# The gated MLP's up projection by seven half-size products instead of eight, its down projection as a phase of its own

## The chip, the cores and the metric

The kernel runs on one core of a Trainium2 chip. The time is device microseconds (us) of one execution of the whole program. The engines of a core are TensorE (PE: matrix products; its weight loads are counted apart as PEld), VectorE (DVE), ScalarE (ACT), GpSimd (POOL) and SyncE (SP), which mostly issues DMAs. Each engine works through its own queue in order.

## The reference, cut to what matters

One decoder block on 512 tokens of 2048 channels: a modulated norm, an input projection, a state-space group and an attention group, an output projection, and then the MLP that the change is about, with a final norm:

```python
def conv_ffn(h, w_up, conv_w, conv_b, w_down):
    up = h @ w_up                                  # (512, 2048) @ (2048, 11264)
    up = causal_depthwise_conv_width_3(up, conv_w) + conv_b
    val, gate = jnp.split(up, 2, axis=-1)          # 5632 channels each
    return (jax.nn.silu(gate) * val) @ w_down      # (512, 5632) @ (5632, 2048)
```

Its result is scaled by a modulation vector (section 5 of the modulation `silu(c) @ w_ada`), added to the residual, and normed.

## The kernel before

All activations lie transposed: channels on 128 partitions, 512 tokens along the row. Every f32 product is made of three matmuls of parts: a number is split into hi (`split`, L59: a cast on ACT) and lo (the difference, on DVE), and `mm3` (L85) adds hi·hi, hi·lo and lo·hi in PSUM (its three lines are L87 to L89). Weights come from memory in pieces of 128 x 2048 (1 MB) by `weights` (L67): one DMA on SP into `wr` (two buffers), then two splits of 128x1024 into `wh` and `wl` (two buffers each). Instructions stand in the order of a scheduler with priorities; the weights' loads and splits are put at high priority, and so ahead. What waits for what follows from buffers: a new tile of a name waits until the last reader of the buffer is done.

Phase C (`phase_c`, L1011) is the second half of the output projection. It adds 16 tiles into the residual `x2` (L1025), sums squares for the norm (`add_square`, L944), and beside it makes section 4 of the modulation: a 1 MB load `adw` (on POOL's queue) and a multiply with sum on DVE (L113) for each of 16 tiles. `norm2` (L1007) makes the norm's factors for each half of the tokens, with a power on POOL (L135).

Phase D (`phase_d`, L1074) is the MLP. `up` makes one of 88 tiles of 128 channels: 16 k-tiles of the contraction, three matmuls each of 512 tokens, so 48 matmuls, then `conv` (L1065: one ACT and two DVE instructions from PSUM). A value tile and its gate tile are a pair; Silu on ACT (L1176) and a product on DVE (L1177) join them, and `split` makes `ah` and `al`, which stay in SBUF. The first pair (`up_first`) runs in halves of 256 tokens while `modulate` (L305: two DVE and one ACT instruction) makes its inputs `h2h` and `h2l`. After every four pairs and one more, `down` adds these four k-tiles into all 16 output tiles: 12 matmuls and one DVE add (L1124) each. So up and down alternate eleven times. Section 5 of the modulation is made beside the early pairs. The last eight output tiles (`last`) run in halves of 256 tokens, so that the norm and the output of one lie beside the products of the other.

## Time and profile before

| | |
|---|---|
| three runs | 2459.17, 2460.2 (median), 2462.0 us |
| the profiled execution: span from first to last instruction | 2464.1 us |
| PE busy | 2336.9 us, 95% of the span |
| DVE, ACT, POOL busy | 61%, 37%, 10% |
| mean granted TensorE clock | 0.967 of full speed |
| DMA | 365 MB, 148 GB/s |

The page gives no other time for the profiled execution than its span, which is 3.9 us above the median of the runs. Phase D takes the time from about 971 us to the end. A matmul's record begins when it starts and ends when its modelled pipeline ends, so neighbours overlap: the pitch from start to start is what a matmul costs, not its record's length.

### The profile page before, as it was taken

What the parts mean: (1) busy time and instruction counts of PE and PEld (TensorE: products, weight loads), DVE (VectorE), ACT (ScalarE), POOL (GpSimd) and SP (SyncE); (2) the same over time, 40 slices, a digit from 0 to 9 for tenths busy, and PEclk for the clock granted to TensorE, in tenths of its full rate; (3) what the DMA queues carried; (4) which work ended last, traced back from release to release, by engine and by line L of the source; (5) the groups of instructions that cost most, each with busy time, mean ns of one, the idle gap of its engine ahead of it and who ended that gap; (6) DMA issues with size and microseconds to landing.
All of it is one profiled execution on the core that took longest, in us unless ns stands there. A gap on an engine that the chain in (4) does not pass through costs nothing.

```text
span 2464.1 us, 27445 instructions
## 1 busy us (share of the span) xinstructions
PE 2336.9 (95%) x10574; PEld 1893.2 (77%) x10574; DVE 1496.3 (61%) x2381; ACT 916.2 (37%) x1602; POOL 251.3 (10%) x313
## 2 busy tenths in 40 slices
PE   7689999989899889999999999999999999999997
PEld 5567778866677668888888888888888888888887
DVE  7688877669988887864443444353434444444437
ACT  3223444458768724322322232222222222222225
POOL 7995111100000010000000000000000000000000
PEclk9899999979899999999999999999999999999999
DMA  8675645576566584642222222222222222222222
GB/s 336 241 242 209 220 144 164 172 221 210 167 228 199 181 307 185 228 182 96 92 100 88 102 86 103 86 103 86 103 86 103 86 103 88 101 88 100 91 98 103
DMA packets 85202, 365.20 MB, mean 148 GB/s; under 512 B 18528, under 2 KB 27104, under 8 KB 51152
## 3 DMA queue, kind: packets, MB, share of 16 engines
q1 hardware_dynamic: 75552, 327.82, 38.1%
q0 software_dynamic: 9520, 35.63, 4.3%
q8 instruction: 83, 1.36, 0.2%
q14 instruction: 47, 0.39, 0.0%
HBM read 341.42 MB, written 21.96 MB: 147 GB/s over the span
## 4 chain that ended last, share of the span: by engine, by line
PE 76%; DVE 8%; POOL 5%; issue 5%; ACT 3%; DMA 2%; SPq 0%; POOLq 0%; DVEq 0%; ACTq 0%
PE up L87 13%; PE up L88 13%; PE up L89 13%; PE dn L87 7%; PE dn L89 7%; PE dn L88 7%; PE mm L87 2%; PE mm L89 2%; PE mm L88 2%; POOL stt L337 2%; DVE adw L113 1%; DVE wl L62 1%; PE s L870 1%; PE acc L629 1%; ACT Pt L882 1%
## 5 line engine op out<-in xcount | busy, mean ns | idle before, releaser
L62 DVE TENSOR_TENSOR wl<-wr,wh 128x1024 fp32r<-128x1024 f32 (+1 forms) x360 | 436.6, 1216 | 552.7 <-ACT wh L62 530.9
L62 ACT CAST wh<-wr 128x1024 fp32r<-128x1024 f32 (+1 forms) x362 | 372.1, 1031 | 1037.1 <-PE up L88 588.3
L88 PE MATMUL up<-h2l,wh 128*128 128x512 f32 x1376 | 543.0, 395 | 0.0
L87 PE MATMUL up<-h2h,wh 128*128 128x512 f32 x1376 | 543.0, 395 | 0.0
L89 PE MATMUL up<-h2h,wl 128*128 128x512 f32 x1376 | 543.0, 395 | 0.0
L88 PEld LDWEIGHTS up<-h2l,wh 128*128 128x128 f32 x1376 | 259.3, 188 | 60.5
L89 PEld LDWEIGHTS up<-h2h,wl 128*128 128x128 f32 x1376 | 259.3, 188 | 60.5
L87 PEld LDWEIGHTS up<-h2h,wh 128*128 128x128 f32 x1376 | 259.3, 188 | 60.3
L89 PE MATMUL dn<-ah,wl 128*128 128x512 f32 (+1 forms) x704 | 274.3, 390 | 0.0
L88 PE MATMUL dn<-al,wh 128*128 128x512 f32 (+1 forms) x704 | 274.2, 389 | 0.0
L87 PE MATMUL dn<-ah,wh 128*128 128x512 f32 (+1 forms) x704 | 274.1, 390 | 0.0
L1124 DVE SCALAR_TENSOR_TENSOR x<-dn,mod,x 128x512 f32<-128x512 f32 (+1 forms) x184 | 133.5, 727 | 188.8 <-PE dn L89 186.7
L135 POOL TENSOR_TENSOR rms_r<-rms_v,mhalf 128x2 f32<-128x2 f32 (+1 forms) x8 | 8.9, 1108 | 1658.7 <-DVE rms_v L133 1658.6
L87 PEld LDWEIGHTS dn<-ah,wh 128*128 128x128 f32 x704 | 132.6, 188 | 29.8 <-ACT ah L62 0.3
L88 PEld LDWEIGHTS dn<-al,wh 128*128 128x128 f32 x704 | 132.6, 188 | 29.6
L89 PEld LDWEIGHTS dn<-ah,wl 128*128 128x128 f32 x704 | 132.6, 188 | 29.6
L113 DVE SCALAR_TENSOR_TENSOR adw<-adw,silc 128x2048 f32<-128x2048 f32 x63 | 149.8, 2377 | 5.7 <-DMA adw<-in_wada_dram 5.7
L87 PE MATMUL mm<-yh,wh 128*128 128x512 f32 (+1 forms) x320 | 129.3, 408 | 17.6 <-ACT yh L62 6.2
L88 PE MATMUL mm<-yl,wh 128*128 128x512 f32 (+1 forms) x320 | 128.1, 401 | 3.9 <-DVE yl L62 3.9
L89 PE MATMUL mm<-yh,wl 128*128 128x512 f32 (+1 forms) x320 | 127.4, 400 | 0.3 <-DVE wl L62 0.3
L87 PE MATMUL b<-hh,wh 128*128 128x512 f32 x192 | 67.7, 409 | 24.2 <-ACT hh L238 14.7
L87 PEld LDWEIGHTS mm<-yh,wh 128*128 128x128 f32 x320 | 62.2, 196 | 32.5 <-ACT yh L62 7.5
(400 smaller groups left out, 3450.9 us busy)
## 6 DMA issues: line engine op xcount, KB each, us to landing
wr<-in_wup_dram SPq DMA_DIRECT2D x88, 1024.0 KB, 4.8
adw<-in_wada_dram SPq DMA_DIRECT2D x49, 1024.0 KB, 6.5
wr<-in_wdn_dram SPq DMA_DIRECT2D x44, 1024.0 KB, 4.8
wr<-in_wada_dram SPq DMA_DIRECT2D x32, 1024.0 KB, 5.0
wr<-in_wout_dram SPq DMA_DIRECT2D x16, 1024.0 KB, 6.0
adw<-in_wada_dram POOLq DMA_DIRECT2D x14, 1024.0 KB, 5.7
wr<-in_wp_dram SPq DMA_DIRECT2D x12, 1024.0 KB, 5.6
s5wt<-in_wuT_dram SPq DMA_DIRECT2D x16, 512.0 KB, 4.2
```

The costliest lines, as they stand in the source:

```text
L62: return self.A.copy(hi, src), self.V.tensor_sub(lo, src, hi.bitcast(F32))
L87: self.T.matmul(ps, wh, xh, start=start, stop=False)
L88: self.T.matmul(ps, wh, xl, start=False, stop=False)
L89: self.T.matmul(ps, wl, xh, start=False, stop=stop)
L113: self.V.scalar_tensor_tensor(t, t, 1.0, self.silc, op0=ALU.mult, op1=ALU.mult, accum_out=out)
L135: self.rms_pow = self.nc.gpsimd.tensor_tensor(r[:, 0:n], v[:, 0:n], self.mhalf.to_broadcast([P, n]), op=ALU.pow)
L337: V.tensor_scalar(w, x, c, None, op0=op0)
L629: T.matmul(Y[:, 64 * g:64 * g + 64], w3[:, :, g], U[:, g], start=True, stop=False)
L870: T.matmul(s[:, :c + n], q[hd], K[b][:, i, k0:k0 + c + n], start=i == 0, stop=i == 1)
L882: A.mul(x, x, rs[:, 3 * hd + 1 + b:3 * hd + 2 + b])
L1124: V.scalar_tensor_tensor(x2[:, m, sl], p[:, sl], self.mod[:, 5, m:m + 1], x2[:, m, sl], op0=ALU.mult, op1=ALU.add)
```

## The change

The up projection of a pair is taken as one matrix product of 2 x 2 blocks: the weights of the value tile and the gate tile (rows), each cut into two halves of the contraction (A11, A12 for the value, A21, A22 for the gate), times the input, cut into halves of the contraction and of the tokens. Pairs 2 to 43 of 0 to 43 make its four result blocks by seven products of 8 k-tiles and 256 tokens (Strassen in Winograd's form), so 7 x 8 x 3 = 168 matmuls of 256 tokens. Four sums of input blocks (`t1` to `t4`) are made once, after pair 0. Four sums of weights are made for each pair on DVE (L1193, in place, 128x1024), each of the seven operands is split, and four DVE instructions put the results together (L1216 to L1219) ahead of the convolution. The gate comes out with its sign turned, which a second set of taps (`tapn`) takes back. Pairs 0 and 1 are made by all eight products, in halves of the tokens.

The gated tile goes to memory (`a_d`) by a DMA on POOL's queue. The residual goes there too in phase C (`x2_d`, sixteen tiles on POOL's queue), since its place is needed. The down projection then follows all of up: five rounds of eight k-tiles and a last one of four, the inputs read back and split again. Section 5 of the modulation is made in its first round. `cv` has three buffers instead of five.

```diff
@@ phase_c
         def add(mt, p, sl):
-            V.scalar_tensor_tensor(x2[:, mt, sl], p, self.mod[:, 2, mt:mt + 1], x2[:, mt, sl],
-                                   op0=ALU.mult, op1=ALU.add)
-            self.add_square(self.acc2[:, sl], x2[:, mt, sl], mt == 0, W)
+            x = x2[mt // 4][:, mt % 4, sl]
+            V.scalar_tensor_tensor(x, p, self.mod[:, 2, mt:mt + 1], x, op0=ALU.mult, op1=ALU.add)
+            self.add_square(self.acc2[:, sl], x, mt == 0, W)
+            nc.gpsimd.dma_start(self.x2_d[:, mt, sl], x)
...
+    def gated(self, m, val, gate, neg, W):
+        val, gate = self.conv(val, m, W), self.conv(gate, NFF + m, W, neg)
+        self.A.activation(gate, gate, AF.Silu)
+        self.V.tensor_mul(val, val, gate)
+        self.nc.gpsimd.dma_start(self.a_d[:, m], val)
...
+    def up_first(self, x2, W, R, ps):
...
+                    if c == 0:
+                        x = x2[k // 4][:, k % 4, sl]
+                        gain, shift = self.mod[:, 4, k:k + 1], self.mod[:, 3, k:k + 1]
+                        self.modulated = self.modulate(x, gain, shift, self.rb2[:, sl], hi, lo, None, x)
+                        A.activation(x, x, AF.Identity, bias=shift)
+                    for e in range(2):
+                        wh, wl = w[k // 8][e]
+                        self.mm3(p[:, 2 * e + f], (wh[:, k % 8], wl[:, k % 8]), (hi, lo), k == 0, k == KT - 1)
...
+    def up_rest(self, ps):
...
+            for c in range(2, NFF):
+                with tc.high_priority():
+                    ra = self.wp.tile([P, 2048], F32, name="wr", bufs=2)
+                    nc.sync.dma_start(ra, a["wup"][c])
+                    rb = W.tile([P, 2048], F32, name="wq", bufs=2)
+                    nc.sync.dma_start(rb, a["wup"][NFF + c])
+                a11, a12, a21, a22 = (r[:, 1024 * i:1024 * i + 1024] for r in (ra, rb) for i in range(2))
...
+                def product(out, src, x, add=None):
+                    with tc.high_priority():
+                        if add is not None:
+                            V.tensor_add(src, src, add)
+                        wh, wl = pair(src)
+                    xh, xl = op[x]
+                    for k in range(8):
+                        self.mm3(out, (wh[:, k], wl[:, k]), (xh[:, k], xl[:, k]), k == 0, k == 7)
+
+                product(sb[:, 2], a11, "b11")
+                p1 = W.tile([P, 256], F32, name="p1", bufs=2)
+                A.copy(p1, sb[:, 2])
+                product(sb[:, 0], a12, "b21")
+                product(sa[:, 0], a22, "t4")
+                product(sa[:, 2], a22, "t1", a21)
+                product(sb[:, 1], a22, "t2", a11)
+                product(sa[:, 3], a12, "b22", a22)
+                product(sa[:, 1], a21, "t3", a11)
...
+                V.tensor_add(e[:, 0::2], sb[:, 0:2], two(p1))
+                V.tensor_add(u, sa[:, 1:3], two(e[:, 2]))
+                V.tensor_add(g, sa[:, 0::2], two(u[:, 0]))
+                V.tensor_add(e[:, 1], sa[:, 3], u[:, 1])
+                self.gated(c, e[:, 0:2].rearrange("p a s -> p (a s)"), g.rearrange("p a s -> p (a s)"), True, W)
+
+    def down(self):
...
+            for q in range(4):
+                nc.sync.dma_start(x2[:, 4 * q:4 * q + 4], self.x2_d[:, 4 * q:4 * q + 4])
...
+            def inputs(k0):
+                r = R.tile([P, 4, S], F32, name="ar", bufs=2)
+                nc.sync.dma_start(r, self.a_d[:, k0:k0 + 4])
...
+                    self.split(r[:, i], ah, al)
...
+            for c in range(5):
+                acts = inputs(8 * c) + inputs(8 * c + 4)
...
+                    for q in range(8):
+                        w = self.weights(a["wdn"][c, q])
                         for e in range(2):
+                            if c == 0:
+                                self.ada_rest(5, 2 * q + e, L, 2)
+                            wh, wl = w[e]
+                            add(2 * q + e, lambda k: (wh[:, k], wl[:, k]), acts, whole)
```

Three places show how the instructions move. First DVE in the middle of the up projection. Before, two tiles of a pair stood there like this (`up` is the tile's bank, `wr` the raw weights):

```order
L62 TENSOR_TENSOR wl<-wr,wh 128x1024 x2
L1070 SCALAR_TENSOR_TENSOR cv<-up,taps,cv 128x511
L1071 SCALAR_TENSOR_TENSOR cv<-up,taps,cv 128x510
L62 TENSOR_TENSOR wl<-wr,wh 128x1024 x2
L1070 SCALAR_TENSOR_TENSOR cv<-up,taps,cv 128x511
L1071 SCALAR_TENSOR_TENSOR cv<-up,taps,cv 128x510
L1177 TENSOR_TENSOR cv<-cv 128x512
L62 TENSOR_TENSOR al<-cv,ah 128x512
```

Now a part of one pair's row on DVE (`xh`, `xl` and `wq` are further buffers of weights; `sa` and `sb` hold the seven results; numbers tell buffers apart):

```order
L1216 TENSOR_TENSOR e_9329<-sb_9126,p1_9155 128x2x256
L62 TENSOR_TENSOR wl_9384<-wr_9347,wh_9383 128x1024
L62 TENSOR_TENSOR xl_9412<-wq_9349,xh_9411 128x1024
L1193 TENSOR_TENSOR wq_9349<-wq_9349 128x1024
L1217 TENSOR_TENSOR u_9330<-sa_9125,e_9329 128x512
L1193 TENSOR_TENSOR wq_9349<-wq_9349,wr_9347 128x1024
L62 TENSOR_TENSOR wl_9441<-wq_9349,wh_9440 128x1024
L1218 TENSOR_TENSOR n_9331<-sa_9125,u_9330 128x512
L1193 TENSOR_TENSOR wq_9349<-wq_9349,wr_9347 128x1024
L1219 TENSOR_TENSOR e_9329<-sa_9125,u_9330 128x256
L1193 TENSOR_TENSOR wr_9347<-wr_9347,wq_9349 128x1024
L62 TENSOR_TENSOR xl_9470<-wq_9349,xh_9469 128x1024
```

The sums and splits of the next pair's weights (9347, 9349) stand between the instructions that put this pair's results together.

Second, SP where up ends and down begins, which is new (`ar` is the gated input, `x2` the residual, both from memory):

```order
L1235 DMA ar_18649<-a_d_77 128x2048
L1230 DMA x2_18625<-x2_d_76 128x2048 x4
L1261 DMA silc_18670<-in_cB_dram 128x2048
L72 DMA wr_18889<-in_wdn_dram 128x2048
L106 DMA adw_18684<-in_wada_dram 128x2048
```

Ahead of this row stand three loads of down weights and the first `ar`. Before, SP's queue held only loads of weights there:

```order
L72 DMA wr_9572<-in_wdn_dram 128x2048
L72 DMA wr_9638<-in_wdn_dram 128x2048
L72 DMA wr_9704<-in_wup_dram 128x2048
L72 DMA wr_9767<-in_wup_dram 128x2048
L72 DMA wr_9836<-in_wup_dram 128x2048
```

Thus the inputs of down have come into SP's queue behind the third load of its weights.

## Rows read from the trace of the kernel before

**Rows 1.** The page's head, its part 1 (busy us, share of the span, instructions of each engine) and the first line of its part 4 (the chain of work that ended last, by engine).

```profile
span 2464.1 us, 27445 instructions
PE 2336.9 (95%) x10574; PEld 1893.2 (77%) x10574; DVE 1496.3 (61%) x2381; ACT 916.2 (37%) x1602; POOL 251.3 (10%) x313
PE 76%; DVE 8%; POOL 5%; issue 5%; ACT 3%; DMA 2%; SPq 0%; POOLq 0%; DVEq 0%; ACTq 0%
```

**Rows 2.** Busy time by stretch: bounds and length in us; busy us (instructions) of PE, PEld, DVE, ACT, POOL; granted clock; DMA share; GB/s. The first stretch is of 512-token matmuls, the others of 256-token ones (the last tiles of down, the last two tiles of the output projection).

```profile
1200.00:1500.00 300.00, 300.00 (x1293) 243.28 (x1292) 132.00 (x148) 79.95 (x93) 0.00 (x0) 1.00 0.27 95
2425.70:2435.70 10.00, 10.00 (x85) 10.00 (x84) 8.18 (x17) 6.83 (x15) 0.00 (x0) 1.00 0.00 0
952.10:960.60 8.50, 8.50 (x72) 8.50 (x71) 4.58 (x8) 3.06 (x5) 0.00 (x0) 1.00 0.67 247
```

**Rows 3.** DVE in order of time amid the up projection: start, length in us, line, operation; in brackets the idle time before and what ended it.

```profile
1199.54 1.22 DVE L62 TENSOR_TENSOR wl<-wr,wh 128x1024 fp32r<-128x1024 f32 x1 [4.34 <-ACT wh L62]
1200.68 0.74 DVE L1070 SCALAR_TENSOR_TENSOR cv<-up,taps,cv 128x511 f32<-128x511 f32 x1
1201.46 0.75 DVE L1071 SCALAR_TENSOR_TENSOR cv<-up,taps,cv 128x510 f32<-128x510 f32 x1
...
1211.84 0.75 DVE L1070 SCALAR_TENSOR_TENSOR cv<-up,taps,cv 128x511 f32<-128x511 f32 x1
...
1223.00 0.74 DVE L1070 SCALAR_TENSOR_TENSOR cv<-up,taps,cv 128x511 f32<-128x511 f32 x1
```

**Rows 4.** Groups of instructions of DVE and ACT from 1100 to 2400 us, shapes apart: count, then busy us, mean ns of one, idle us before and what ended it.

```profile
L62 DVE TENSOR_TENSOR wl<-wr,wh 128x1024 fp32r<-128x1024 f32 x234 | 286.7, 1225 | 502.0 <-ACT wh L62 494.2
L1124 DVE SCALAR_TENSOR_TENSOR x<-dn,mod,x 128x512 f32<-128x512 f32 x156 | 117.1, 751 | 185.0 <-PE dn L89 183.5
L1071 DVE SCALAR_TENSOR_TENSOR cv<-up,taps,cv 128x510 f32<-128x510 f32 x77 | 57.6, 748 | 2.4
L62 DVE TENSOR_TENSOR al<-cv,ah 128x512 fp32r<-128x512 f32 x38 | 26.2, 690 | 19.9 <-ACT ah L62 19.9
L62 ACT CAST wh<-wr 128x1024 fp32r<-128x1024 f32 x233 | 244.3, 1049 | 850.4 <-PE up L88 538.9 <-PE dn L88 311.5
L1069 ACT ACTIVATE cv<-up,taps 128x512 f32<-128x512 f32 x77 | 59.6, 774 | 0.0
L1176 ACT ACTIVATE cv<-cv 128x512 f32<-128x512 f32 x38 | 24.0, 632 | 86.5 <-DVE cv L1071 86.5
L62 ACT CAST ah<-cv 128x512 fp32r<-128x512 f32 x38 | 23.5, 619 | 22.0 <-DVE cv L1177 22.0
```

**Rows 5.** PE in order of time: the first and the last of 120 matmuls of 256 tokens in a row, and two that follow on an interruption.

```profile
2425.70 0.28 PE L87 MATMUL dn<-ah,wh 128*128 128x256 f32 x1
...
2439.87 0.28 PE L89 MATMUL dn<-ah,wl 128*128 128x256 f32 x1
...
2440.36 0.37 PE L87 MATMUL dn<-ah,wh 128*128 128x256 f32 x1
2440.56 0.28 PE L88 MATMUL dn<-al,wh 128*128 128x256 f32 x1
```

**Rows 6.** DVE in order of time while the first pair's inputs are modulated, the first of its two instructions for each of three tiles by row.

```profile
984.23 1.26 DVE L308 SCALAR_TENSOR_TENSOR cv<-x,mod,rb 128x256 f32<-128x256 f32 x3
...
986.60 1.27 DVE L308 SCALAR_TENSOR_TENSOR cv<-x,mod,rb 128x256 f32<-128x256 f32 x3
```

**Rows 7.** ACT in order of time in the same place, three tiles by row.

```profile
984.73 1.31 ACT L309 ACTIVATE h2h<-cv,mod 128x256 fp32r<-128x256 f32 x3 [1.06 <-DVE cv L308]
```

**Rows 8.** Phase C: busy time in one stretch, columns as in rows 2.

```profile
880.00:940.00 60.00, 57.75 (x239) 46.18 (x240) 53.85 (x68) 15.49 (x19) 5.92 (x11) 0.96 0.81 300
```

**Rows 9.** POOL in order of time: the issue of one DMA in phase C.

```profile
870.91 0.59 POOL L106 DMA_DIRECT2D adw<-in_wada_dram  x1 [7.82 <-DVE mod L317]
```

**Rows 10.** Busy time in the stretches around a stall of PE, columns as in rows 2.

```profile
875.00:880.00 5.00, 1.83 (x10) 1.53 (x8) 4.04 (x5) 1.99 (x2) 0.54 (x1) 0.51 0.67 247
880.00:885.00 5.00, 3.51 (x8) 2.81 (x9) 5.00 (x9) 1.26 (x2) 0.36 (x1) 0.50 0.93 324
885.00:890.00 5.00, 5.00 (x22) 4.03 (x21) 3.26 (x5) 1.06 (x2) 0.71 (x2) 0.96 0.98 375
```

**Rows 11.** PE in order of time behind that stall, 512-token matmuls.

```profile
881.49 0.76 PE L87 MATMUL mm<-yh,wh 128*128 128x512 f32 x1 [4.66 <-DVE x L1025]
882.05 0.63 PE L88 MATMUL mm<-yl,wh 128*128 128x512 f32 x1
882.48 0.63 PE L89 MATMUL mm<-yh,wl 128*128 128x512 f32 x1
```

**Rows 12.** The page's DMA issues: count, KB each, median us from issue to landing.

```profile
adw<-in_wada_dram SPq DMA_DIRECT2D x49, 1024.0 KB, 6.5
wr<-in_wdn_dram SPq DMA_DIRECT2D x44, 1024.0 KB, 4.8
```

**Rows 13.** The page's group of the modulation's products on DVE, columns as in rows 4.

```profile
L113 DVE SCALAR_TENSOR_TENSOR adw<-adw,silc 128x2048 f32<-128x2048 f32 x63 | 149.8, 2377 | 5.7 <-DMA adw<-in_wada_dram 5.7
```

More of the change, by code (lines that the diff above doesn't have):

```diff
@@ L46 @@
 ADA = [2, 2, 2, 2, 2, 2, 2, 2, 2, 2, 2, 2, 2, 2, 2, 2]
-CVB = 5
+CVB = 3
 M_K, M_C = 0, 512
@@ L109, in ada @@
             self.after([load], self.heads)
-        if sec == 5:
-            self.after([load], self.modulated)
         with self.tc.high_priority(-120 if late else 0):
@@ L1189, in phase_d @@
-            down(*pend)
+            x2 = H.tile([P, KT, S], F32, name="x2")
+            for q in range(4):
+                nc.sync.dma_start(x2[:, 4 * q:4 * q + 4], self.x2_d[:, 4 * q:4 * q + 4])
+            acc = H.tile([P, S], F32, name="acc2")
+            def inputs(k0):
+                r = R.tile([P, 4, S], F32, name="ar", bufs=2)
+                nc.sync.dma_start(r, self.a_d[:, k0:k0 + 4])
+                out = []
+                for i in range(4):
+                    ah, al = (R.tile([P, S], F32R, name=n, bufs=12) for n in ("ah", "al"))
+                    self.split(r[:, i], ah, al)
+                    out.append((ah, al))
+                return out
@@ new lines, in add @@
+            def add(m, w, acts, sl, end=False):
+                p = ps.tile([P, 4, P], F32, name="dn", bufs=6).rearrange("p a b -> p (a b)")[:, sl]
+                n = len(acts)
+                for k in range(n):
+                    self.mm3(p, w(k), [x[:, sl] for x in acts[k]], k == 0, k == n - 1)
+                x = x2[:, m, sl]
+                V.scalar_tensor_tensor(x, p, self.mod[:, 5, m:m + 1], x, op0=ALU.mult, op1=ALU.add)
+                if end:
+                    self.add_square(acc[:, sl], x, m == 0, H)
+                    A.mul(x, x, self.vec(V_GFIN + m))
@@ new lines, in down, with quad @@
+            acts = inputs(40)
+            E = st.enter_context(tc.tile_pool(name="po", bufs=1, reuse_waits="tile"))
+            def quad(w, e):
+                wh, wl = w[e // 2]
+                return lambda k: (wh[:, 4 * (e % 2) + k], wl[:, 4 * (e % 2) + k])
+            for q in range(2):
+                w = self.weights(a["wdl"][q])
+                for e in range(4):
+                    add(4 * q + e, quad(w, e), acts, whole, True)
+            w = [self.weights(a["wdl"][2])]
+            w.append(self.weights(a["wdl"][3], E.tile([P, 4, 8, P], F32R, name="wz")))
@@ new lines, in down, with norm, final @@
+            out = E.tile([P, KT, S], F32, name="out")
+            rb = [None, None]
+            def norm(f):
+                so = slice(256 * f, 256 * f + 256)
+                rb[f] = H.tile([P, S], F32, name="cv", bufs=CVB)[:, 0:256]
+                A.copy(rb[f], self.rms(acc[:, so], C_INVD, ps, "up", 2, 2))
+            def final(f):
+                so = slice(256 * f, 256 * f + 256)
+                k0 = 0
+                for n in ((2,) * 8 if not f else (2, 2, 4, 4, 2, 2)):
+                    k = slice(k0, k0 + n)
+                    V.tensor_mul(out[:, k, so], x2[:, k, so], rb[f].unsqueeze(1).to_broadcast([P, n, 256]))
+                    nc.sync.dma_start(a["out"][:, k, so], out[:, k, so])
+                    k0 += n
@@ L1191, in run @@
+            for f in range(2):
+                for e in range(8):
+                    if f and e == 2:
+                        norm(0)
+                    add(8 + e, quad(w[e // 4], e % 4), acts, slice(256 * f, 256 * f + 256), True)
+            norm(1)
+            final(0)
+            final(1)
     def run(self):
```

241 lines of the change are left out of this document (121 added, 120 removed).

## The prediction

> **What bounds the kernel now.** I read the page's head and chain first: PE holds 76% of the chain that ended last, and is busy 95% of a span of 2464.1 us [rows 1]. Then the busy time by stretch: from 1200 to 1500 us PE is busy 300.00 of 300.00 us at clock 1.00, DVE 132.00, ACT 79.95, DMA share 0.27 [rows 2]. So in the MLP nothing waits ahead of PE, and what counts is the pitch of its matmuls. The convolution's instruction L1070 comes once for each tile of 48 matmuls, at 1200.68, 1211.84 and 1223.00 us [rows 3]: 11.16 us for 48, a pitch of 0.2325 us at 512 tokens. For 256 tokens I take a run of 120 matmuls: the first starts at 2425.70, the last at 2439.87 [rows 5], so 14.17 / 119 = 0.1191 us. In the other such stretch 72 starts fill 8.5 us plus the part of one that hangs over [rows 2], about 0.120. I use 0.1195, with 0.119 and 0.120 as bounds.
>
> **Pairs 2 to 43, the gain.** A pair costs PE 2 x 11.16 = 22.32 us now. Seven products of 8 x 3 matmuls of 256 tokens cost 168 x 0.1195 = 20.08 us (19.99 to 20.16). The gain is 2.24 us a pair, 42 x 2.24 = **94 us** (91 to 98). Seven eighths of the columns would be 19.53; the rest is the dearer half-length matmul.
>
> This holds if DVE keeps up, since its cover shrinks most. By pair it does 7 differences and 4 sums of 128x1024 at 1.225 us = 13.5; four results, three of 512 and one of 256 elements, about 3 x 0.75 + 0.42 = 2.7; four convolution steps at 0.748 = 3.0; one product 0.69 [rows 4]. That is 19.9 us by full durations, against 20.08 of PE. But back to back they overlap: L62 starts at 1199.54 and the next instruction at 1200.68 [rows 3], 1.14 instead of 1.22, which makes 11 x 1.14 = 12.5 and 18.8 in all, 94%. ACT does 7 casts at 1.049, two convolution starts at 0.774, Silu 0.632 and a copy of about 0.4, 9.9 us [rows 4].
>
> DVE works in order, so I follow its row from the moment 0 at which a pair's seventh product ends, with 24 x 0.1195 = 2.87 us a product. The first result that waits for that product (u) stands behind the next pair's third split and first sum. The weights' buffers hold four products, so the third split's cast waits for the sixth product of the pair before, which ends at -2.87: cast to -1.8, split to -0.6, sum to +0.6. So u comes 0.6 us late; nothing on PE waits for it. From there 18.8 - 2.3 = 16.5 us of work are left, to 17.1; the next such cast is there at 20.08 - 1.8 = 18.3. DVE therefore waits about a microsecond in each pair and doesn't fall behind. The fourth product's weights are split at about 3.2 us and wanted at 3 x 2.87 = 8.6: five microseconds of slack, which every later one keeps too. I forecast PE as the bound, DVE with almost no room.
>
> [...]
>
> **Pairs 0 and 1, phase C.** Pair 1 now takes 192 matmuls at 0.1195 = 22.9 instead of 22.3: **+0.6**. Pair 0 is paced by its inputs. DVE takes 2.37 us for three tiles [rows 6]; ACT took 1.31 for three [rows 7] and now does a second instruction on each, 2.6 for three. Over 32 tiles that is up to 32 x 0.08 = 2.6 us; the last ones can come late, and the splits of pair 1's weights now stand behind two new DVE instructions of 1.14 us. I take **+2** (0 to 5). In phase C 4 MB of residual more go to memory. The stretch 880 to 940 moved 300 GB/s at a share of 0.81 [rows 8], so full use would be about 370 GB/s and 4 MB take 11 us, as much as the idle 0.19 x 60 = 11. POOL spends 0.59 us on an issue [rows 9], and one such issue stands ahead of the first half's power for the norm. DVE, at 53.85 of 60, waits for the `adw` loads that share the DMAs. I take **+2** (0 to 8).
>
> **Pair 1 to pair 2.** Here buffers couple the engines. Pair 2's first split needs the buffer that pair 1 reads to its end (0 here). Cast 1.05, split 1.23: the first matmul with the lo weights can start at 2.4, and product 1 ends at 5.2. The second cast stands on ACT behind Silu of pair 1, which waits for four convolution steps on DVE, which stand behind that first split: 2.4 + 4 x 0.77 = 5.5, Silu to 6.2, cast to 7.2, split to 8.4. So PE waits 2.4 and then 3.2; from there PE's 2.87 a product stays behind what is ready. With the clock (below) **+6.5** (3 to 12).
>
> **Up to down.** T is the end of the last up product. SP's queue now has, in this order, the third load of down weights, then the two loads of inputs (`ar`), then the residual. The third load needs the first one's buffer; the second half of that is split into a buffer that product 6 holds to T - 2.87. Cast and split end at about T - 0.5, so `ar` is issued at about T. Where loads queue up a landing takes 6.5 us, alone 4.8 [rows 12]. DVE has its last convolution in front of it until about T + 7.5 anyway. Cast 0.62 and difference 0.69 [rows 4] give a first complete k-tile at about T + 8; then DVE's 0.69 a tile keeps PE's 3 x 0.2325 = 0.70. Bounds: 4.8 + 0.6 = 5, and two loads in a row, 9.6 + 1.3 = 11.
>
> [...] Some 3.5 us at half speed lose 1.75: I take 2 here (0 to 6), so **+10** for this boundary (5 to 17).
>
> **The down phase.** It has the same number of matmuls, and fewer DVE adds (6 instead of 11 a tile), which were covered. Its first round is 384 x 0.2325 = 89 us. Section 5 of the modulation now falls in it: 16 x 2.38 = 38.1 on DVE [rows 13], with 16 splits at 1.23 = 19.7, 16 adds at 0.75 = 12, 8 input differences at 0.69 = 5.5 [rows 4], in all 75: covered, if the loads come. About 10 MB stand ahead of the first modulation load, some 30 us at the rate above, while six banks hold results for 6 x 5.58 = 33 us, from T + 8 to T + 41. I take **+1** (0 to 8). The end of the kernel is as before.
>
> **Sum.** -94 + 0.6 + 2 + 2 + 6.5 + 10 + 1 = -72 us. Against the profiled execution: 2464 - 72 = 2392. The median of the runs is 3.9 lower: **2388 us**. By the favourable ends -98 + 0.6 + 0 + 0 + 3 + 5 + 0 = -89, 2371; by the others -91 + 0.6 + 5 + 8 + 12 + 17 + 8 = -40, 2420.
>
> **Rivals.**
> - *DVE sets the pace without being slower than before.* At full durations 19.9 plus the wait of a microsecond or more for the third cast: 21.2 a pair. For it: 94% leave nothing for a longer instruction. Against: the overlap in rows 3, and the slack of five microseconds. Time: 42 x 1.1 = 47 more, 2435.
> - *Slower: casts and differences in lockstep.* If the four sums each leave DVE waiting for the cast that follows (1.05), a pair takes 19.9 + 4.2 = 24.1 us, 42 x 1.8 = 75 above 22.32; with the 22 us of the other terms 2460 + 97 = 2557. It turns from gain to loss at a pair of 22.32 - 22/42 = 21.8 us. Against: in the new row of DVE other work stands between each sum and its split.
> - *The boundaries cost twice as much:* PE stays at the lower clock after both stalls, or the burst of 10 MB starves the first round. 22 becomes 50: 2416. For it: a clock of 0.5 for ten microseconds in rows 10.
> - *The boundaries cost nearly nothing:* 2371, if the loads land sooner than rows 12 say.
> - *The gain is not there because weight loads stay exposed.* At the 0.20 of rows 5 a pair takes 168 x 0.20 = 33.6: 42 x 11.3 = 474 more than before, 2950 with the other terms. Three stretches in rows 2 and 5 speak against it. [...]
>
> **Chances.** The forecast (pairs at PE's pitch, boundaries near 22 us) 0.71; boundaries at twice that 0.10; DVE's pace 0.10; lockstep 0.04; boundaries for nothing 0.04; exposed loads 0.01. The range 2370 to 2425 holds the first two, the fifth and the better part of the third's lower cases, and leaves out the losses. A change of less than 0.2% (5 us) can't be told from none here: faster 0.94, same 0.01, slower 0.05.
>
> **What would show it.** Right: matmuls of 256 tokens with a pitch of 0.12 from about 1030 us on, u (L1217) every 20.1 us, PE busy throughout, DVE above 90%; one gap of some 8 us on PE about 845 us later, ended by `ah` or `al`; two of 2 to 3 us at the start of pair 2. Wrong: u every 20.5 us or more with PE waiting for L62 on DVE; a pitch well above 0.12; a clock under 1.00 in the pairs; PE waiting for `dn` banks in the first round of down.

## The result and the profile after

The changed kernel took 2394.16 us (median of 4 runs, 2393.2 to 2398.66), the kernel before 2460.14 us beside it on the same chip: a ratio of 0.9728, 95% interval 0.9707 to 0.975. The forecast was 2388 us (2370 to 2425), faster. In the terms of its sum the profiled span fell from 2464.1 to 2396.9 us, by 67 instead of 72. That the sum comes out so near is partly luck, since errors of both signs offset each other; the experiments below are about these.

The head, part 1 and the chain's first line of the page of the changed kernel, against [rows 1]:

```profile
span 2396.9 us, 34691 instructions
PE 2244.6 (94%) x13694; PEld 1967.3 (82%) x13694; DVE 1865.8 (78%) x2776; ACT 1084.3 (45%) x1807; POOL 288.5 (12%) x375
PE 71%; DVE 11%; issue 6%; POOL 5%; ACT 4%; DMA 3%; SPq 0%; POOLq 0%; DVEq 0%; ACTq 0%
```

PE is busy 92.3 us less, with 3120 more (and shorter) matmuls; the span fell by only 67.2, since waits came with the change. Busy time by stretch shows which (columns as in [rows 2]): the pairs, phase C, the start of pair 2, the change from up to down, steady down.

```profile
1200.00:1500.00 300.00, 299.94 (x2529) 297.01 (x2528) 274.15 (x302) 144.86 (x166) 8.14 (x15) 1.00 0.33 119
880.00:940.00 60.00, 53.96 (x220) 42.97 (x221) 52.61 (x66) 15.15 (x19) 12.02 (x22) 0.91 0.87 325
1040.00:1050.00 10.00, 9.22 (x65) 8.92 (x66) 9.72 (x9) 4.84 (x7) 0.00 (x0) 0.83 0.07 28
1880.00:1900.00 20.00, 15.03 (x53) 11.71 (x54) 9.67 (x14) 7.80 (x13) 0.54 (x1) 0.74 0.91 374
2000.00:2300.00 300.00, 300.00 (x1287) 241.38 (x1286) 120.49 (x132) 70.44 (x78) 0.00 (x0) 1.00 0.32 109
```

In the pairs PE is busy all the time at clock 1.00 while DVE is at 91%: DVE keeps up. But PEld, which loads weights and was never idle in the 256-token stretches of [rows 2], is idle for 3 us of 300. Phase C lost 3.8 us of PE's time in 60 against [rows 8].

DVE in order of time in the pairs, the counterpart of [rows 3]; the first result that waits for the seventh product (u, L1217) marks each pair:

```profile
1399.25 0.68 DVE L1217 TENSOR_TENSOR u<-sa,e 128x512 f32<-128x512 f32 x1
...
1416.74 1.23 DVE L62 TENSOR_TENSOR xl<-wq,xh 128x1024 fp32r<-128x1024 f32 x1 [1.49 <-ACT xh L62]
...
1419.15 0.68 DVE L1217 TENSOR_TENSOR u<-sa,e 128x512 f32<-128x512 f32 x1
...
1436.78 1.23 DVE L62 TENSOR_TENSOR wl<-wq,wh 128x1024 fp32r<-128x1024 f32 x1 [1.65 <-ACT wh L62]
...
1439.18 0.68 DVE L1217 TENSOR_TENSOR u<-sa,e 128x512 f32<-128x512 f32 x1
```

u comes every 19.9 and 20.0 us, and DVE's one wait in a pair is where the prediction put it, before the third split, 1.5 to 1.65 us long.

PE's visible waits from the start of the pairs to the start of down, in order of time:

```profile
1032.49 0.39 PE L87 MATMUL sb<-b11h,wh 128*128 128x256 f32 x1 [0.66 <-ACT wh L62]
1033.75 0.39 PE L89 MATMUL sb<-b11h,wl 128*128 128x256 f32 x1 [0.76 <-DVE wl L62]
1040.43 0.42 PE L87 MATMUL sb<-b21h,xh 128*128 128x256 f32 x1 [3.79 <-ACT p L1201]
1041.42 0.58 PE L89 MATMUL sb<-b21h,xl 128*128 128x256 f32 x1 [0.35 <-DVE xl L62]
1884.97 0.79 PE L87 MATMUL dn<-ah,wh 128*128 128x512 f32 x1 [7.60 <-ACT ah L62]
```

The stretches, in us, from the starts of PE's first and last matmuls in each. The run called again is a second profile of the changed kernel; the last two columns belong to experiments below.

| stretch | before | changed | again | t4_second | all_five |
|---|---|---|---|---|---|
| start of pair 0 | 972.3 | 982.8 | 977.4 | 977.5 | 973.2 |
| pairs 0 and 1 | 47.7 | 49.7 | 49.9 | 49.9 | 49.5 |
| pair 2 | 22.3 | 26.8 | 28.3 | 25.7 | 22.2 |
| each of pairs 3 to 43 | 22.32 | 19.95 | 19.95 | 19.60 | 19.60 |
| last up start to first down start | none | 7.9 | 7.9 | 7.9 | 4.2 |
| first to last down start | about 491.7 | 496.9 | 495.8 | 495.7 | 508.2 |
| profiled span | 2464.1 | 2396.9 | 2392.4 | 2375.4 | 2375.4 |

(Before, up and down alternate; its 491.7 is 2016 matmuls at 0.2325 and 192 at 0.1195. The pairs are (last up start - start of pair 3) / 41; in the changed kernel (1877.10 - 1059.33) / 41.)

### The profile page after: what moved, and what is told of

Read it like the earlier page. It is cut to its first block, busy times and chain, and to the rows that moved or that the text cites. A ratio compares the mean times of both kernels' runs of the same rounds, so it can differ in the third digit from the quotient of the medians.

```text
span 2396.9 us, 34691 instructions
## 1 busy us (share of the span) xinstructions
PE 2244.6 (94%) x13694; PEld 1967.3 (82%) x13694; DVE 1865.8 (78%) x2776; ACT 1084.3 (45%) x1807; POOL 288.5 (12%) x375
## 4 chain that ended last, share of the span: by engine, by line
PE 71%; DVE 11%; issue 6%; POOL 5%; ACT 4%; DMA 3%; SPq 0%; POOLq 0%; DVEq 0%; ACTq 0%
PE dn L88 7%; PE dn L87 7%; PE dn L89 7%; PE sa L89 7%; PE sa L87 7%; PE sa L88 7%; PE sb L87 5%; PE sb L89 5%; PE sb L88 5%; PE mm L87 2%; PE mm L89 2%; PE mm L88 2%; DVE wl L62 2%; DVE adw L111 1%; PE s L870 1%
## 5 line engine op out<-in xcount | busy, mean ns | idle before, releaser
L62 ACT CAST wh<-wr 128x1024 fp32r<-128x1024 f32 (+1 forms) x257 | 261.9, 1024 | 519.7 <-PE dn L88 331.6
L62 DVE TENSOR_TENSOR wl<-wr,wh 128x1024 fp32r<-128x1024 f32 (+1 forms) x255 | 307.2, 1209 | 68.6 <-ACT wh L62 47.7
L1249 DVE SCALAR_TENSOR_TENSOR x<-dn,mod,x 128x512 f32<-128x512 f32 (+1 forms) x104 | 73.2, 707 | 203.4 <-PE dn L89 202.8
L88 PEld LDWEIGHTS dn<-al,wh 128*128 128x128 f32 x704 | 132.8, 189 | 29.6 <-DVE al L62 0.4
L62 ACT CAST wh<-wq 128x1024 fp32r<-128x1024 f32 x84 | 88.0, 1048 | 137.6 <-DVE wq L1193 101.0
L62 ACT CAST xh<-wq 128x1024 fp32r<-128x1024 f32 x84 | 88.5, 1054 | 135.8 <-DVE wq L1193 100.8
L1082 POOL DMA_DIRECT2D a_d<-cv x44 | 23.9, 543 | 879.4 <-DVE cv L1081 879.4
L62 DVE TENSOR_TENSOR wl<-wq,wh 128x1024 fp32r<-128x1024 f32 x84 | 102.4, 1220 | 33.1 <-ACT wh L62 33.1
L62 DVE TENSOR_TENSOR xl<-wq,xh 128x1024 fp32r<-128x1024 f32 x84 | 102.5, 1220 | 31.4 <-ACT xh L62 31.4
L1193 DVE TENSOR_TENSOR wq<-wq,wr 128x1024 f32<-128x1024 f32 x84 | 102.1, 1216 | 0.1
L62 ACT CAST xh<-wr 128x1024 fp32r<-128x1024 f32 x63 | 65.8, 1044 | 47.0 <-issue 19.9
```

What stands on the lines that cost most here:

```text
L62: return self.A.copy(hi, src), self.V.tensor_sub(lo, src, hi.bitcast(F32))
L88: self.T.matmul(ps, wh, xl, start=False, stop=False)
L1082: self.nc.gpsimd.dma_start(self.a_d[:, m], val)
L1193: V.tensor_add(src, src, add)
L1249: V.scalar_tensor_tensor(x, p, self.mod[:, 5, m:m + 1], x, op0=ALU.mult, op1=ALU.add)
```

## The experiments

All are edits of the changed kernel, each timed against the kernel before on the same chip. That one's median was 2461.5 to 2464.6 us there, so the ratios are what to compare.

| run | ratio (95%) | span of the profile |
|---|---|---|
| again (no edit) | 0.9734 (0.9716 to 0.9752) | 2392.4 |
| eight | 1.0141 (1.0122 to 1.0159) | 2493.3 |
| eight_busy | 1.0124 (1.0092 to 1.0157) | 2491.6 |
| dve2 | 0.9720 (0.9685 to 0.9755) | 2392.3 |
| dve5 | 0.9995 (0.9974 to 1.0015) | 2461.4 |
| t4_second | 0.9654 (0.9639 to 0.9669) | 2375.4 |
| x2_unwritten | 0.9716 (0.9694 to 0.9737) | 2384.6 |
| x2_late | 0.9705 (0.9690 to 0.9719) | 2388.0 |
| halves_moved | 0.9706 (0.9691 to 0.9720) | 2391.7 |
| cv_apart | 0.9707 (0.9666 to 0.9748) | 2395.2 |
| acts_early | 0.9728 (0.9710 to 0.9746) | 2392.5 |
| all_five | 0.9655 (0.9636 to 0.9673) | 2375.4 |

### The pairs: is it the products that saved the time?

**eight** undoes the seven products alone, with the sums, the copy and the four result instructions that belong to them.

```diff
-                product(sb[:, 2], a11, "b11")
...
-                product(sa[:, 1], a21, "t3", a11)
+                w = []
+                for src in (a11, a12, a21, a22):
+                    with tc.high_priority():
+                        w.append(pair(src))
+                for i in range(4):
+                    for j in range(2):
+                        wh, wl = w[2 * (i // 2) + j]
+                        xh, xl = op[(("b11", "b21"), ("t3", "b22"))[i % 2][j]]
+                        for k in range(8):
+                            self.mm3(sa[:, i], (wh[:, k], wl[:, k]), (xh[:, k], xl[:, k]),
+                                     j == 0 and k == 0, j == 1 and k == 7)
```

> Pairs 2 to 43 by eight products of halves instead of seven (192 matmuls of 256 tokens, four splits, no sums of weights, no recombination); two phases, memory and everything else as in the changed kernel. Theory (TensorE sets the pace of both forms): each pair takes 192 x 0.1188 = 22.8 us against 19.95, so the median is 2394 + 42 x 2.86 = 2514 (2505 to 2520), that is, slower than the kernel before by some 50 us, which is what the two phases and the halves of tokens cost without the seventh of the products saved. Rival (VectorE or the chain of sums and casts holds the seven-product form above its matmuls): the eight-product form runs at a shorter pitch than 0.1188, so that a pair takes 22.3 or less and the median is below 2495.

A stretch of its pairs, and two splits one pair apart on DVE:

```profile
1200.00:1500.00 300.00, 300.00 (x2573) 300.00 (x2572) 112.13 (x119) 82.95 (x92) 7.06 (x13) 1.00 0.31 107
```

```profile
1199.14 1.22 DVE L62 TENSOR_TENSOR wl<-wr,wh 128x1024 fp32r<-128x1024 f32 x1 [1.91 <-ACT wh L62]
...
1221.54 1.22 DVE L62 TENSOR_TENSOR wl<-wr,wh 128x1024 fp32r<-128x1024 f32 x1 [1.91 <-ACT wh L62]
```

A pair takes 22.40 us, a pitch of 22.40 / 192 = 0.1167, and the median was 2497.36. That the products save the time is shown: without them the kernel is 1.4% slower than before. But 2505 to 2520 was wrong, and so was the theory in its plain form: with the same matmuls the pitch is 0.1167 where nothing but products and splits is done, and 0.1187 (19.95 / 168) with seven products. At 0.1167 a pair of seven would take 19.60. The rival's bound of 22.3 wasn't reached either, but its sense was right: 0.35 us a pair, 15 us in all, are lost to something.

**eight_busy** asks whether that is DVE's traffic. It is eight with sixteen more operations per pair on DVE:

```diff
+        for _ in range(16 if m > 1 else 0):
+            self.V.tensor_sub(gate, val, gate)
         self.nc.gpsimd.dma_start(self.a_d[:, m], val)
```

> The eight-product form with 16 more VectorE operations of 128x512 per pair (about 0.61 us each, 9.8 us per pair, on the gate's buffer after it was read), on which nothing waits: VectorE about 80% busy instead of 38%. The eight-product run took 22.40 us a pair, a pitch of 0.1167 against 0.1188 in the seven-product form. Theory (the traffic of VectorE slows TensorE's reads): the pair grows to 22.6 to 22.8 us (pitch 0.1177 to 0.1188), the median by 8 to 17 us. Rival (the longer pitch of the seven-product form comes from short waits at its seven product edges, not from VectorE's load): the pair stays at 22.40 and the median within 3 us of the eight-product run's.

```profile
1200.00:1500.00 300.00, 300.00 (x2574) 300.00 (x2573) 257.08 (x338) 82.83 (x92) 7.03 (x13) 1.00 0.31 107
```

DVE is 86% busy instead of 37%, and a pair still takes 192 x 300 / 2574 = 22.4 us: 2574 matmuls start in 300 us instead of 2573. The traffic theory falls; what is left is a wait.

**t4_second** looks for it. The trace of the changed kernel names one, in the view of the copy of the first product out of PSUM (L1201): who waited for it, in us, how often.

```profile
  PEld sb L87: 12.2, 42
```

Once in each pair the first weight load of the b21 product stands until ScalarE has copied the b11 product, because both products are written to the tile `sb`. (In PE's row four matmuls of the t4 product already stand between the two. Of the 12.2 us, 4.0 fall in pair 2; the other 41 waits are 0.2 us each.) PE's own row hides it behind the matmul in flight (299.94 busy of 300). The edit lets another product run meanwhile:

```diff
                 product(sb[:, 2], a11, "b11")
                 p1 = W.tile([P, 256], F32, name="p1", bufs=2)
                 A.copy(p1, sb[:, 2])
-                product(sb[:, 0], a12, "b21")
                 product(sa[:, 0], a22, "t4")
+                product(sb[:, 0], a12, "b21")
```

> Only the second and third products change places (a22 with t4 before a12 with b21). In the changed kernel the b21 product waits once per pair for ScalarE to copy the first product out of PSUM (0.20 us in the weight loads' row). Theory (that wait is part of the 0.35 us per pair by which seven products are slower than the eight-product form's pitch): pairs take 19.7 to 19.8 us instead of 19.95, the median falls by 6 to 10 us. Rival (another wait takes its place, since t4's weights are now wanted earlier): 19.95 or more, no change.

```profile
1200.00:1500.00 300.00, 300.00 (x2573) 300.00 (x2573) 280.39 (x307) 147.09 (x168) 8.67 (x16) 1.00 0.35 126
```

PEld is never idle now, and the count of matmuls is that of eight. Pairs take (1856.50 - 1053.10) / 41 = 19.60 us. So the one wait accounts for all of the 0.35 us, more than its own 0.2, and the expectation was too small. By the starts of PE's matmuls in the changed kernel, the two steps beside b21's first matmul take 0.28 and 0.22 us where others take about 0.12, some 0.26 us too much; the rest lies in the steps that follow. The ratio is 0.9654 against 0.9734 for the unedited kernel (again, below), some 20 us. The two profiles differ by 17.0, of which 41 x 0.354 = 14.5 come from the pairs and 2.5 from pair 2.

### How much room DVE has

**dve2** and **dve5** add two and five operations per pair, where eight_busy adds 16:

```diff
+        for _ in range(2 if neg else 0):
+            self.V.tensor_sub(gate, val, gate)
         self.nc.gpsimd.dma_start(self.a_d[:, m], val)
```

> The changed kernel with two more VectorE operations of 128x512 per pair (about 1.2 us) on the gate's buffer after it was read. Theory (TensorE sets the pace and VectorE has 1.5 to 1.66 us to spare per pair): pairs stay within 0.1 us of 19.95, the median within 5 us of the changed kernel. Rival (the chain of casts, sums and recombination runs in step with the products, so that VectorE's work sets the pace): +1.2 us a pair, +51 us.

> Five such operations per pair (about 3.05 us). Theory (spare time of 1.5 to 1.66 us): pairs take 21.3 to 21.6 us, the median rises by 57 to 70 us to about 2455 to 2465, VectorE near 100% busy. Rival (in step from the first): 23.0 a pair, +128 us. Third (more spare time than the trace shows as idle): under +40.

Stretches of the pairs, first of dve2, then of dve5:

```profile
1200.00:1500.00 300.00, 299.94 (x2534) 297.01 (x2534) 291.47 (x333) 143.95 (x166) 8.10 (x15) 1.00 0.33 119
```

```profile
1200.00:1500.00 300.00, 287.90 (x2365) 283.32 (x2364) 294.12 (x352) 134.35 (x154) 7.57 (x14) 0.98 0.31 111
```

Two are free: pairs of (1872.21 - 1056.23) / 41 = 19.90, DVE at 97%. Five are not: (1927.07 - 1059.43) / 41 = 21.16 on the mean. That mean mixes two stretches, by the starts of the pairs. Pairs 3 to 10 still take 19.94, while DVE falls behind (the results have two sets of buffers). From pair 16 on most pairs still take about 20 us, but every third or fourth takes 24.2 to 25.0, and the mean is 21.64. There an added 3.05 costs 1.7 us, so about 1.4 us were spare; the trace showed 1.5 to 1.65 idle. PE is the bound in the changed kernel, and the lockstep rival falls (it wanted 1.2 us already for two). The median fits the theory's 57 to 70 us for a second reason: the pairs give 42 x 1.2 = 51, and the rest was lost in the first round of down, where PE now waited. Its longest wait there:

```profile
1984.90 0.77 PE L87 MATMUL dn<-ah,wh 128*128 128x512 f32 x1 [13.12 <-DVE x L1251]
```

SyncE's row of dve5 shows where it comes from, though the five operations end with the pairs:

```profile
1927.45 17.84 SPq L1237 DMA_DIRECT2D ar<-a_d  x4
...
1974.31 0.90 SPq L106 DMA_DIRECT2D adw<-in_wada_dram  x2
```

The order of the loads has changed there: four loads of inputs instead of two, and more loads of weights, stand ahead of the first modulation loads, which go out 1974.31 - 1935.47 = 38.8 us after the first matmul of down, and 1901.64 - 1884.97 = 16.7 us in the changed kernel. DVE waits for them, and PE for DVE.

### Phase C: what made it late

DVE in order of time, the first product of phase C that waits for a modulation load, in the kernel before and in the changed one:

```profile
876.11 2.29 DVE L113 SCALAR_TENSOR_TENSOR adw<-adw,silc 128x2048 f32<-128x2048 f32 x1 [0.96 <-DMA adw<-in_wada_dram]
```

```profile
879.57 2.29 DVE L111 SCALAR_TENSOR_TENSOR adw<-adw,silc 128x2048 f32<-128x2048 f32 x1 [3.15 <-DMA adw<-in_wada_dram]
```

Two causes offer themselves: the 4 MB of writes (from 885 us on, that is behind this first wait), and SyncE's first two modulation loads, which go out later behind the load of weights ahead of them. SyncE's row of the kernel before, then of the changed one:

```profile
851.57 0.33 SPq L72 DMA_DIRECT2D wr<-in_wout_dram  x1
851.95 0.90 SPq L106 DMA_DIRECT2D adw<-in_wada_dram  x2
```

```profile
852.86 0.33 SPq L72 DMA_DIRECT2D wr<-in_wout_dram  x1
857.10 0.83 SPq L106 DMA_DIRECT2D adw<-in_wada_dram  x2
```

It is 4.2 us instead of 0.4, and 4.2 to 4.3 in every profile of a changed kernel. Their buffers lie in another pool now (`Wa`), and SyncE waits there for a matmul of the attention group (what it waited for, us, times, longest):

```profile
SPq L106 <- PE tp L902: 3.9, 1, 3.9
```

**x2_unwritten** leaves out the writes (down then reads the residual's old value), **x2_late** makes them in four large pieces, three behind the last modulation load and one behind the last tile:

```diff
-            nc.gpsimd.dma_start(self.x2_d[:, mt, sl], x)
...
+        for q in range(3):
+            self.after([nc.gpsimd.dma_start(self.x2_d[:, 4 * q:4 * q + 4], x2[q])], self.last_load)
...
+        nc.gpsimd.dma_start(self.x2_d[:, 12:], x2[3])
```

> Left out: the 14 writes of the new x2 to DRAM in the output projection (4 MB); the down phase reads the old x of the same shape instead, so the output lacks the output projection in the residual. Theory A (the writes take bandwidth from the modulation weights, which then land late and hold VectorE and through it TensorE): the last two output-projection tiles start 4 to 5 us earlier than in the changed kernel (about 956, not 960.6), median 2388 to 2391. Theory B (the delay comes from the first modulation loads, which start at 857.1 instead of 852.0 because their buffers moved onto other memory, and is carried through): no change, 960 and 2393 to 2396. Theory C (the writes sit ahead of the modulation loads on GpSimd's queue, 0.55 us each): also about 956, but then moving them to another queue must do the same as leaving them out.

> The same 4 MB of x2 are written, but as four pieces of 1 MB on the same queue, three of them only after the last modulation load, the fourth after the last tile. Theory A (bandwidth): like leaving the writes out, last tiles at about 956, median 2388 to 2391, unless the first modulate of the up phase then waits for a piece still being read (that would show as a wait of ActE or VectorE on DMA at 972 to 985). Theory B (later first loads carried through): 960, 2393 to 2396.

**again** is the changed kernel once more:

> The changed kernel once more, to see how far its output projection varies by itself: the last two output-projection tiles began at 960.6 in its first profile, and at 954.0 to 959.3 in five runs whose program is the same up to there. If the writes cost a fixed 8 us, it is 957 to 961 again; if most of the 8.5 us was that run's own, 954 to 957. Ratio to the kernel before 0.971 to 0.974.

DVE's waits for these loads between 862 and 965 us, and the start of the last two tiles of the output projection, from the span's start and from the load `wr` shown above:

| run | waits, us in all | the first of them | last two tiles from | counted from `wr` |
|---|---|---|---|---|
| before | 5.0 | 1.0 | 952.1 | 100.5 |
| changed | 9.5 | 3.2 | 960.6 | 107.8 |
| again | 8.0 | 3.3 | 955.2 | 103.8 |
| seven other runs with the same program up to there | 7.8 to 9.4 | 3.0 to 4.3 | 948.6 to 959.3 | 103.8 to 106.3 |
| x2_late | 6.2 | 3.7 | 953.1 | 102.2 |
| all_five (writes late too) | 4.8 | 3.1 | 952.5 | 101.7 |
| x2_unwritten | 4.7 | 4.0 | 949.4 | 102.0 |

The median landing of the modulation loads on GpSimd's queue goes with it, between 862 and 955 us; in turn the kernel before, the changed one, x2_late and x2_unwritten:

```profile
adw<-in_wada_dram POOLq DMA_DIRECT2D x14, 1024.0 KB, 5.7
```

```profile
adw<-in_wada_dram POOLq DMA_DIRECT2D x14, 1024.0 KB, 6.9
```

```profile
adw<-in_wada_dram POOLq DMA_DIRECT2D x14, 1024.0 KB, 5.4
```

```profile
adw<-in_wada_dram POOLq DMA_DIRECT2D x14, 1024.0 KB, 5.3
```

The writes are one cause; the late loads very likely are the other. The load `wr` itself goes out anywhere from 844.8 to 854.6 us in the nine profiles of this program, a scatter that comes from the stages ahead; counted from it, the last two tiles start 105.1 us on in the mean, 4.5 later than in the one profile of before. Where the writes are out of the way it is 101.7 to 102.2, below every one of the nine: the writes cost about 3 us. The 1.2 to 1.7 us that remain against before go with the loads that start later; no run moved the `adw` buffers back alone.

How these loads act shows in the first wait, which stays at 3 to 4 us whether x2 is written or not. DVE doesn't wait for the two late loads themselves: they land by 866.78 in the changed kernel, and DVE takes them up at 869.29. But the four loads of the residual's old value stand behind them and land 3 us later (the last 24.2 us after `wr` instead of 21.2), and the third modulation load, issued 19.4 us after `wr` as before, lands after 7.1 to 8.4 us instead of 5.2. The later waits sum to 4 to 6 us with the writes in their place and to 0.7 to 2.5 without. In x2_late nothing on DVE or ACT then waits for a piece still being read. Bandwidth (theory A) and the place in GpSimd's queue (theory C) aren't told apart by this, as both edits take the writes out of the way of both; the landing time speaks for the former. In the time of the whole kernel it isn't settled: the ratios of 0.9716 and 0.9705 stand 4 to 7 us below again's 0.9734, with intervals that overlap. The start of the last two tiles varies by 12 us between profiles of one and the same program, 4 us of it counted from `wr`, and again was at 955.2, within the second of the two cases expected of it. The 8.5 us of the first profile were partly that run's own: the mean of the nine such profiles is 956.0, 3.9 behind the one profile of before.

### The start of pair 2

**halves_moved** lays the second set of weight halves over x2 instead of over the convolution buffers of pairs 0 and 1; **cv_apart** also gives these buffers a pool of their own, whereupon the scheduler puts pair 2's casts ahead of pair 1's convolutions.

```diff
-            for n, d in (("e", 3), ("u", 2), ("n", 2)):
-                W.tile([P, d, 256], F32, name=n, bufs=1 if n == "u" else 2)
+            for n in ("xh", "xl"):
+                W.tile([P, 8, P], F32R, name=n, bufs=2)
+            W.tile([P, 2048], F32, name="wq", bufs=2)
...
-        o = W.tile([P, S], F32, name="cv", bufs=CVB)
+        o = self.cvp.tile([P, S], F32, name="cv", bufs=CVB)
```

> Only the order of the places of the second pool of the up phase is changed: the second set of weight halves and the second raw weight buffer lie over x2, whose last reader is the split for t3 at 1030.5, and no longer over the convolution buffers of pairs 0 and 1, whose last reader ends at 1039. Theory (memory: the second cast of pair 2 waits for the place of the convolution buffer): the gap of 3.79 us in pair 2 goes to 0.5 or less, pair 2 takes 21 to 22.5 us instead of 26.84, the median falls by 4 to 6 to about 2389. Rival (queue: ScalarE and VectorE are simply busy with the convolutions of pair 1, in order): pair 2 stays at 25.5 or more, 2393 to 2395.

> The places as in halves_moved, and the convolution buffers in a pool of their own that outlives the change of pools, so that the casts of pair 2 needn't stand behind the convolutions of pair 1 in ScalarE's and VectorE's queues. halves_moved took only 0.9 us from the gap of 3.8 us. Theory (the order in the two queues makes the rest): pair 2 takes 21 to 22.5 us instead of 26.84, the clock there stays above 0.9, the median falls 4 to 6 us below the changed kernel. Rival (the loads of pair 2's weights, issued at 1010.8 and 1026.9, come too late whatever the order): pair 2 stays at 25 or more.

PE's waits there, first halves_moved, then cv_apart:

```profile
1036.83 0.39 PE L87 MATMUL sb<-b21h,xh 128*128 128x256 f32 x1 [2.92 <-ACT p L1205]
```

```profile
1027.49 0.39 PE L87 MATMUL sb<-b11h,wh 128*128 128x256 f32 x1 [1.33 <-ACT wh L62]
1028.94 0.39 PE L89 MATMUL sb<-b11h,wl 128*128 128x256 f32 x1 [0.95 <-DVE wl L62]
...
1888.15 0.80 PE L87 MATMUL dn<-ah,wh 128*128 128x512 f32 x1 [4.46 <-ACT ah L62]
```

The memory theory accounts for 0.9 us of the gap, which went only from 3.79 to 2.92. The order in the queues was the rest: in cv_apart the gap is gone and pair 2 takes 1049.17 - 1027.49 = 21.7 us, as expected, 5.2 less than in the changed kernel and 6.6 less than in again. The span didn't follow (2395.2), since the new pool changed the order of SyncE's loads at the start of down, too: the second load of inputs now stands behind the residual's, and PE waits 4.46 us for it at 1888.15; down took 1874.88 to 2379.90, 9 us more than in again. The ratio is not below that of halves_moved.

### From up to down, and all edits together

**acts_early** puts the two input loads ahead of the third load of down weights.

```diff
-                        w = self.weights(a["wdn"][c, q])
+                        w = self.weights(a["wdn"][c, q], behind=self.acts if (c, q) == (0, 2) else None)
...
-                acts = inputs(8 * c) + inputs(8 * c + 4)
+                with tc.high_priority() if c == 0 else ExitStack():
+                    acts = inputs(8 * c) + inputs(8 * c + 4)
```

> The first two loads of the down phase's inputs stand ahead of the third down weight load on SyncE's queue and the whole of their splitting has high priority. Theory (the gap of 7.75 us between the phases is the wait of that load behind the weight load, then its landing of some 6 us): the loads go out at about 1869 instead of 1877.4, and the gap falls to 3.5 to 5.5 us, the rest being the casts that stand behind the last pair's recombination in ScalarE's queue; median 2 to 4 us lower. Rival (the recombination and convolution of the last pair alone make the gap): 7 or more.

PE's waits between 1845 and 2030 us of that run (what it waited for, us, times, longest):

```profile
PE dn L89 <- DVE mod L323: 5.2, 1, 5.2
PE dn L89 <- ACT ah L62: 3.9, 1, 3.9
PE dn L90 <- DVE al L62: 1.7, 1, 1.7
```

The loads go out as the last products run, at 1858.90 us, and the gap is 1871.08 - 1866.91 = 4.2 instead of 7.9, so the queue made almost half of it. The rest is the cast behind the last pair's convolutions. But 1.7 us follow at the second operand, and 5.2 more where a result of the first round waits for a modulation load that now stands behind other loads (the first go out 29.6 us after the first matmul of down instead of 15.7 in again). Down takes 506.2 us instead of 495.8. The ratio, 0.9728, isn't told from that of again.

**all_five** is x2_late, cv_apart (with halves_moved), acts_early and t4_second in one kernel.

> x2_late, halves_moved with cv_apart, acts_early and t4_second together. If they add: x2 writes 5, pair 2 5, boundary 2 to 4, pairs 6 to 10 us below the changed kernel, so a ratio to the kernel before of 0.963 to 0.966 against 0.973. If the writes late or the other order at the down phase's start give part back: 0.967 to 0.970.

The ratio lies where adding would put it, but for another reason, as the table of stretches shows: against again it gains 4.2 before pair 0 (with the scatter of phase C), 6.1 in pair 2, 14.5 in the pairs and 3.7 in the gap, and gives 12.4 back in down, where PE waits 1.4 us for the second operand and twice 2.9 us behind a modulation load, as in acts_early. t4_second alone is as fast. A kernel with t4_second, x2_late and pair 2 mended, but down's loads in the old order, wasn't run.

## Why the prediction was right, and where it was not

- **Pairs 2 to 43, the gain of 94 us: mis-sized, by two errors that offset.** At the pace of pairs 3 to 43 the gain was 42 x 2.37 = 99.5. The term "168 x 0.1195" took the pitch from tiles at the end of down and in the output projection [rows 2, 5]; where nothing waits it is 0.1167 in the pairs (eight, t4_second), 0.5 us a pair less. Half of the pairs' weights lie in `xh` and `xl`, where a matmul comes every 0.113 us, and half in `wh` and `wl`, where it is 0.120 as in those tiles (last section). And no wait between the products was counted: b21 waits for the copy of b11, 0.35 us a pair. I had counted the copy in ACT's work, not as something that PE waits for. That 19.95 us a pair came so near to 20.08 is luck.
- **DVE almost without room, PE the bound: right.** 91 to 94% busy, one wait of 1.5 to 1.65 us before the third split (forecast about a microsecond), room for two operations of 0.6 us (dve2) and about 1.4 us in the steady part of dve5. The rivals with DVE's pace and with lockstep fell by dve2.
- **Weight loads don't stay exposed: right.** In t4_second 2573 matmuls of 128*128 and 256 tokens, each with a load, start in 300 us, 0.117 us apart and not 0.20. What the loads row does show is that a load that has to wait can cost time though PE's row looks full: the 0.35 us a pair that t4_second mended.
- **Pairs 0 and 1, +2.6: right** (2.0 to 2.2).
- **Phase C, +2 (0 to 8): too small.** The start of pair 0 came 10.5 us later in the first profile and 5.1 in the second, of which 1.3 and -0.1 lie ahead of the load `wr`. The step that failed is the one that weighed only the writes against idle DMA time: they cost about 3 us although the share was below 1 (0.87 from 880 to 940 us), and 1.2 to 1.7 more go, untested by itself, with a part of the change that the prediction didn't price at all, the move of the `adw` buffers, which delays the first two loads by 3.9 us and the residual's behind them by 3.
- **Pair 1 to pair 2, +6.5 (3 to 12): right**, in size (6.9 and 8.3 above a pair at the new pace) and in cause: the second cast behind Silu of pair 1, shown by cv_apart. What ended the wait was the copy of b11, which stands right behind that cast on ACT. Of the two waits the first was smaller (0.66 and 0.76 instead of 2.4) and the second larger (3.79 instead of 3.2). The 0.9 us that the forecast adds to these two waits for the clock no run shows; in the changed kernel ten steps from 1041.80 to 1043.93 took 0.21 us each, at a granted clock of 0.50 from 1041 to 1044.
- **Up to down, +10 (5 to 17): right.** The gap is 7.9 us, and with a granted clock of 0.74 from 1880 to 1900 about 2.8 more by the starts of the first matmuls (1.9 in again). The 2 us of the forecast for the clock, from 3.5 us at half speed, no run shows: in the changed kernel the first 12 steps took 1890.55 - 1884.97 = 5.58 us, at a granted clock of 0.50 from 1885 to 1889, where 12 x 0.2331 is 2.80. `ar` stands behind the third load of weights, as forecast, and DVE's and ACT's last convolution behind that: acts_early took away the first and 4.2 us remained.
- **Down, +1 (0 to 8): somewhat too small**, 4 to 5 with the boundary's clock, 2 to 3 without. Nothing waits in the first round; PE's matmuls simply come at 300 / 1287 = 0.2331 instead of 300 / 1293 = 0.2320 in [rows 2]. Over 2016 matmuls that is 2.2 us. The cause wasn't tried.
- **Two sums of the prediction.** Twice the boundaries' 22 us is 44, not 50, so that rival's time is 2410, not 2416; DVE's work back to back adds up to 18.9, not 18.8. No forecast hung on either.

## What to carry to other kernels

Here a product was saved in full only where PE never waited at its edges (19.60 us a pair against 19.95): look at the row of the weight loads too, since a wait of 0.2 us behind a busy PE cost 0.35 us in every pair. The copy out of PSUM did no harm a product away from the next write to the same tile (t4_second). And where a stage is tuned by the order of its loads, moving a buffer or a load changes that order for others: cv_apart and acts_early each mended their own place and gave it back in down (9 and 10 us more than in again), and part of what dve5 lost was lost in this way (a wait of 13.12 us in down).

## What was not expected of the hardware

- In the profile of eight, matmuls of the same shape come at two paces, by the tile that holds their weights: PE in order of time with weights in `xh` and `xl`, then in `wh` and `wl`.

```profile
1199.90 0.28 PE L89 MATMUL sa<-b22h,xl 128*128 128x256 f32 x1
...
1200.58 0.28 PE L89 MATMUL sa<-b22h,xl 128*128 128x256 f32 x1
1200.70 0.28 PE L87 MATMUL sa<-b11h,wh 128*128 128x256 f32 x1
...
1202.02 0.28 PE L89 MATMUL sa<-b11h,wl 128*128 128x256 f32 x1
```

  0.68 us for six steps, 0.113 each, against 1.32 for eleven, 0.120 each. In that run each operand meets only one of the two kinds of tile. In t4_second each meets both, in turn from pair to pair. The b22 product there, in one pair and in the next:

```profile
1499.78 0.28 PE L88 MATMUL sa<-b22l,wh 128*128 128x256 f32 x1
...
1500.98 0.28 PE L89 MATMUL sa<-b22h,wl 128*128 128x256 f32 x1
...
1517.90 0.28 PE L87 MATMUL sa<-b22h,xh 128*128 128x256 f32 x1
...
1519.94 0.28 PE L87 MATMUL sa<-b22h,xh 128*128 128x256 f32 x1
```

  1.20 us for ten steps against 2.04 for eighteen. By the starts of all matmuls of pairs 3 to 42 it is 0.120 against 0.113 for each of the seven operands, and so in the changed kernel too, but for the products around the wait. So it goes with the tile of the weights. The tiles lie in different pools; with `xh` and `xl` laid elsewhere, in halves_moved, the two paces were the same (0.113 and 0.120). What makes the difference stays open. It is large enough (0.113 against 0.120 us) to make a pitch taken from one place of a kernel wrong for another.
- A wait of 0.2 us of one weight load per pair cost 0.35 us (t4_second).
- VectorE at 86% instead of 37% left the pace of the matmuls as it was, 22.4 us for 192 (eight_busy).
- The start of the last output-projection tiles varied from 948.6 to 960.6 us between profiles of the same program up to there; counted from SyncE's load of weights 100 us earlier, by 4.0 us.
